# 615 products more on TensorE, in 41 patterns, that nothing reads

## The chip, the cores and the metric

The kernel runs on one core of one Trainium2 chip. The metric is the device time of one execution in microseconds. Two timed executions took 1457.32 and 1456.70 us, median 1457.01. A third was recorded by the hardware profiler.

In the profile PE is TensorE, the engine of matrix products, and PEld its weight loads; DVE is VectorE, ACT is ScalarE, POOL is GpSimd and SP is SyncE, which here only issues DMAs. A product on TensorE has a stationary operand, which a weight load brings into the array first, and a moving operand, whose columns are streamed through; the result is added up in PSUM.

## The reference

A trunk of two layers works on 272 tokens (16 learned ones and 256 real ones) of width 2048. Each layer ends in a residual and a layer norm.

```
for layer in range(DEPTH):                 # DEPTH = 2
    if layer % 2 == 0:
        f = _even_mixer(h, ...)            # gated linear attention and stick-breaking attention
    else:
        f = _odd_mixer(h, ...)             # Mamba-2 SSD mixer
    h = _layer_norm(DEEPNORM_ALPHA * h + f, ln_g[layer], ln_b[layer])
return h[:, PREFIX:]                       # the 256 real tokens
```

Both mixers are one wide input projection (2048 to some ten thousand columns), the mixing itself, a gate, and an output projection back to 2048. All of it is in float32. Most of the arithmetic is in the projections.

## The kernel before, in words

**Products.** A float32 operand is split into two parts, hi (rounded to the type fp32r, in which TensorE takes one pass over the columns) and lo (the rest). Every projection product is three products: hi times hi, hi times lo and lo times hi. The helper `three` (L161 to L165) issues them with the weights as stationary operand: `whi` with `xhi`, `whi` with `xlo`, `wlo` with `xhi`. So the first two have the same weights, and the moving operand has up to 272 columns, one per token. `out1_half` (L411 to L423), for the last output projection, does it the other way round: the activations `yh` and `yl` are stationary, and 512 (or 256) columns of weights are streamed.

**Operands.** `xhi` and `xlo` hold the layer's input for all 16 blocks of 128 input columns, 288 elements a row and block (`XW`), in fp32r. The weights come as units of 128 x 2048 elements by DMA into `raw`, three buffers; ACT makes `whi` of half a unit (L145), DVE or POOL makes `wlo` (L146), five buffers each. `self.parts[i, h]` names the parts of half h of unit i. `NU` is the number of units, so `NU - 1` is the last one.

**PSUM.** Four banks (`pj`) take the projections, two (`po`, L158 to L159) all smaller products in turn, and two (`zb`) serve the attention scores.

**Order.** The program is written as a list of units. While a unit's products are issued, generators for the mixing of earlier units are stepped on (`tick`), so that their instructions come in between. The order of each engine's instructions is then set by a planner, which goes by a simulated timeline and by priorities (program order, with some instructions marked as urgent): it takes the first instruction in priority that is ready. Waits between engines follow from what each instruction reads and writes. Each engine works off its own list in order.

**The end.** `tail` (L1087 to L1143) does the last four units by itself. The second and third of these are split not into `whi` and `wlo` but into the buffers of `xhi` and `xlo` (L1099, L1100), which nobody needs as input any more: elements 0 to 4095 of each row. The last unit is split as usual. Then come eight blocks of products, for two groups of 128 tokens and four groups of 512 output columns; DVE adds each block to the residual (L430) and takes its statistics (L1122). After the last block the second group of tokens is normalised on DVE, ACT and POOL (L1126 to L1141) and written out by three DMAs (L1142, L1143).

`setup` issues ten products of `ones` with `ones` before the first data is there (L231); nothing reads their result.

Of the kernel before, what the change touches and what calls it, by code (L numbers as in the profile page):

```python
# [12 lines left out]
P = 128  # L13
# [53 lines left out]
NU = len(L0) + len(L1)  # L67
# [20 lines left out]
class _Body:  # L88
# [998 lines left out]
    def tail(self):  # L1087

        nc, lp = self.nc, self.lp
        vec, pool = nc.vector, nc.gpsimd  # L1090
        i0, g = NU - 4, NG - 1
        self.drain()
        self.load_unit(i0 + 2)
        for n, dq in enumerate((1, 2)):
            for h in range(2):
                src = self.raw[i0 + dq][:, h * 1024 : (h + 1) * 1024]
                o = slice((2 * n + h) * 1024, (2 * n + h + 1) * 1024)
                hi, lo = [a.rearrange("p k t -> p (k t)")[:, o] for a in (self.xhi, self.xlo)]
                nc.scalar.activation(hi, src, AF.Copy)  # L1099
                vec.tensor_tensor(lo, src, hi.bitcast(F32), op=ALU.subtract)  # L1100
                self.parts[i0 + dq, h] = (hi, lo)
            if n == 0:
                self.load_unit(i0 + 3)
        lg = self.hp.tile([P, D], F32, tag="hacc", name="lg")
        lb = lp.tile([P, D], F32, tag="M", name="lb")
        nc.sync.dma_start(lg, self.lnr_d[0].partition_broadcast(P))
        nc.sync.dma_start(lb, self.lnr_d[1].partition_broadcast(P))
        for h in range(2):
            self.split_half(i0 + 3, h)
        for t in range(2):  # L1110
            st = lp.tile([P, 8, 6], F32, tag="fst", name=self.nm("fst"), bufs=2)
            acc = self.acc[:, t, :]
            for dq in range(4):
                halves = (0, 1) if t == 1 and dq == 3 else (None,)
                for b in halves:
                    ps = self.pj()
                    for h in range(2):
                        self.out1_half(ps, g, t, *self.parts[i0 + dq, h], h, b)
                    self.out1_add(ps, g, t, dq, b)
                    with self.tc.high_priority():  # L1120
                        for c in range(2) if b is None else (b,):
                            vec.bn_stats(st[:, 2 * dq + c, :], acc[:, dq * 512 + c * 256 : dq * 512 + (c + 1) * 256])  # L1122
            mv = lp.tile([P, 2], F32, tag="fmv", name=self.nm("fmv"), bufs=2)
            v, r, tm, mr = [lp.tile([P, 1], F32, tag=f"f{n}", name=self.nm("f"), bufs=2) for n in range(4)]
            with self.tc.high_priority():
                vec.bn_aggr(mv, st)  # L1126
                vec.tensor_scalar(v, mv[:, 1:2], LN_EPS, None, op0=ALU.add)
                nc.scalar.activation(r, v, AF.Ln)
                nc.scalar.activation(r, r, AF.Exp, scale=-0.5)
                self.newton(r, v, tm)  # L1130
                vec.scalar_tensor_tensor(mr, mv[:, 0:1], -1.0, r, op0=ALU.mult, op1=ALU.mult)
            cut = (0, 1024, 2048) if t == 0 else (0, 384, 1216, 2048)
            ch = [slice(a, b) for a, b in zip(cut, cut[1:])]
            for cs in ch[1:]:
                vec.scalar_tensor_tensor(acc[:, cs], acc[:, cs], mv[:, 0:1], lg[:, cs], op0=ALU.subtract, op1=ALU.mult)
            a = acc[:, ch[0]]
            nc.scalar.activation(a, a, AF.Identity, bias=mr, scale=r)
            pool.tensor_tensor(a, a, lg[:, ch[0]], op=ALU.mult)
            pool.tensor_tensor(a, a, lb[:, ch[0]], op=ALU.add)
            for cs in ch[1:]:  # L1140
                vec.scalar_tensor_tensor(acc[:, cs], acc[:, cs], r, lb[:, cs], op0=ALU.mult, op1=ALU.add)  # L1141
                nc.sync.dma_start(self.out[t * P : (t + 1) * P, cs], acc[:, cs])  # L1142
            nc.sync.dma_start(self.out[t * P : (t + 1) * P, ch[0]], a)  # L1143


def _pack(i):
# [53 lines left out]
```

## Time and profile before

| | us |
|---|---|
| median of two runs | 1457.01 |
| the profiled execution | 1456.58 |
| its span, first to last instruction | 1454.5 |
| PE busy | 1434.3 |
| DVE busy | 983.0 |
| ACT busy | 760.9 |
| POOL busy | 339.3 |

The granted clock of TensorE was 0.998 of full speed on average. A row of the timeline gives the start in us from the span's beginning, the length, the engine, the line, the operation, what it writes and reads with shapes, and how many it stands for. A group row gives the busy time and the mean length of one instruction in ns. Products overlap: the next starts before the last has ended. A row of the windows gives a stretch of the span, its length, and the busy time of each engine in it, with the number of instructions that lie in it at least partly.

### The profile page before, as it was taken

What the parts mean: (1) busy time and instruction counts of PE and PEld (TensorE: products, weight loads), DVE (VectorE), ACT (ScalarE), POOL (GpSimd) and SP (SyncE); (2) the same over time, 40 slices, a digit from 0 to 9 for tenths busy, and PEclk for the clock granted to TensorE, in tenths of its full rate; (3) what the DMA queues carried; (4) which work ended last, traced back from release to release, by engine and by line L of the source; (5) the groups of instructions that cost most, each with busy time, mean ns of one, the idle gap of its engine ahead of it and who ended that gap; (6) DMA issues with size and microseconds to landing.
All of it is one profiled execution on the core that took longest, in us unless ns stands there. A gap on an engine that the chain in (4) does not pass through costs nothing.

```text
span 1454.5 us, 26054 instructions
## 1 busy us (share of the span) xinstructions
PE 1434.3 (99%) x10780; PEld 1358.5 (93%) x10780; DVE 983.0 (68%) x1510; ACT 760.9 (52%) x1123; POOL 339.3 (23%) x297
## 2 busy tenths in 40 slices
PE   9999999999999999999989999999999999999997
PEld 7999999999999999999989999899898998989975
DVE  8646575574564454446897889577876767768677
ACT  6535454454335544445587566555555555555541
POOL 4000000000101010013502125433333433434323
PEclk9999999999999999999999999999999999999999
DMA  7644544444444444543435654554554555444551
GB/s 260 207 169 149 174 146 165 154 149 171 162 157 168 138 139 171 184 135 127 145 132 176 253 192 163 203 213 164 210 173 163 205 177 218 149 173 171 203 203 58
DMA packets 36566, 249.82 MB, mean 172 GB/s; under 512 B 4128, under 2 KB 4960, under 8 KB 7776
## 3 DMA queue, kind: packets, MB, share of 16 engines
q1 hardware_dynamic: 36304, 247.90, 48.5%
q8 instruction: 84, 1.38, 0.4%
q14 instruction: 34, 0.28, 0.1%
q10 hardware_dynamic: 144, 0.26, 0.1%
HBM read 245.94 MB, written 2.20 MB: 171 GB/s over the span
## 4 chain that ended last, share of the span: by engine, by line
PE 93%; DVE 4%; issue 1%; ACT 1%; POOL 1%; DMA 0%; POOLq 0%; SPq 0%; DVEq 0%
PE pj L163 24%; PE pj L165 24%; PE pj L164 23%; PE pj L421 4%; PE pj L423 4%; PE pj L422 4%; DVE wlo L146 1%; PE po L1053 1%; DVE xlo L735 1%; PE po L1055 1%; PE po L1007 1%; PE po L1057 0%; ACT whi L145 0%; DMA raw<-in_wts 0%; DVE hacc L836 0%
## 5 line engine op out<-in xcount | busy, mean ns | idle before, releaser
L163 PE MATMUL pj<-xhi,whi 128*128 128x272 f32 (+3 forms) x2560 | 738.9, 289 | 4.9 <-DVE fix L811 2.9
L165 PE MATMUL pj<-xhi,wlo 128*128 128x272 f32 (+3 forms) x2560 | 738.0, 289 | 0.0
L164 PE MATMUL pj<-xlo,whi 128*128 128x272 f32 (+3 forms) x2560 | 733.0, 286 | 1.9 <-DVE xlo L829 1.9
L146 DVE TENSOR_TENSOR wlo<-raw,whi 128x1024 fp32r<-128x1024 f32 (+1 forms) x402 | 511.6, 1275 | 301.1 <-ACT whi L145 298.6
L145 ACT ACTIVATE whi<-raw 128x1024 fp32r<-128x1024 f32 (+1 forms) x432 | 452.5, 1049 | 424.3 <-PE pj L164 358.3
L163 PEld LDWEIGHTS pj<-xhi,whi 128*128 128x128 f32 x2560 | 480.8, 188 | 9.2 <-issue 3.2
L164 PEld LDWEIGHTS pj<-xlo,whi 128*128 128x128 f32 x2560 | 482.0, 188 | 3.9 <-DVE xlo L829 2.4
L165 PEld LDWEIGHTS pj<-xhi,wlo 128*128 128x128 f32 x2560 | 480.8, 188 | 2.3 <-issue 1.5
L163 PE MATMUL pj<-mixh,whi 128*128 128x272 f32 x384 | 112.2, 294 | 0.0
L164 PE MATMUL pj<-mixl,whi 128*128 128x272 f32 x384 | 111.3, 290 | 0.0
L165 PE MATMUL pj<-mixh,wlo 128*128 128x272 f32 x384 | 110.9, 289 | 0.0
L146 POOL TENSOR_TENSOR wlo<-raw,whi 128x1024 fp32r<-128x1024 f32 x30 | 74.2, 2474 | 140.2 <-ACT whi L145 140.2
L421 PE MATMUL pj<-whi,yh 128*128 128x512 f32 (+1 forms) x244 | 98.2, 402 | 0.0
L423 PE MATMUL pj<-whi,yl 128*128 128x512 f32 (+1 forms) x244 | 96.0, 393 | 0.0
L422 PE MATMUL pj<-wlo,yh 128*128 128x512 f32 (+1 forms) x244 | 95.6, 392 | 0.0
L252 POOL TENSOR_TENSOR gr<-gr,gsc 128x1088 f32<-128x1088 f32 x6 | 15.4, 2574 | 294.8 <-ACT gsc L251 294.8
L163 PEld LDWEIGHTS pj<-mixh,whi 128*128 128x128 f32 x384 | 72.1, 188 | 0.5
L164 PEld LDWEIGHTS pj<-mixl,whi 128*128 128x128 f32 x384 | 72.3, 188 | 0.3
L165 PEld LDWEIGHTS pj<-mixh,wlo 128*128 128x128 f32 x384 | 72.3, 188 | 0.1
L430 DVE SCALAR_TENSOR_TENSOR acc<-pj,rr,acc 128x512 f32<-128x512 f32 (+1 forms) x65 | 47.4, 737 | 30.3 <-PE pj L423 30.3
L1061 POOL TENSOR_TENSOR yu<-yu,gz 128x256 f32<-128x256 f32 x32 | 39.2, 1233 | 80.0 <-DVE yu L1060 79.8
L423 PEld LDWEIGHTS pj<-whi,yl 128*128 128x128 f32 x244 | 46.0, 188 | 10.6
(302 smaller groups left out, 1507.6 us busy)
## 6 DMA issues: line engine op xcount, KB each, us to landing
raw<-in_wts SPq DMA_DIRECT2D x214, 1024.0 KB, 4.8
ebc<-edr SPq DMA_DIRECT2D x8, 1664.0 KB, 6.5
hacc<-in_xT SPq DMA_DIRECT2D x8, 272.0 KB, 6.4
raw<-in_wts SPq DMA_DIRECT2D x8, 256.0 KB, 5.4
lg<-in_lnr SPq DMA_DIRECT2D x1, 1024.0 KB, 4.3
lb<-in_lnr SPq DMA_DIRECT2D x1, 1024.0 KB, 6.0
out_h<-acc SPq DMA_DIRECT2D x2, 512.0 KB, 2.6
out_h<-acc SPq DMA_DIRECT2D x2, 416.0 KB, 2.5
```

The costliest lines, as they stand in the source:

```text
L145: self.nc.scalar.activation(hi, src, AF.Copy)
L146: eng.tensor_tensor(lo, src, hi.bitcast(F32), op=ALU.subtract)
L163: mm(ps, whi, xhi, start=first, stop=False)
L164: mm(ps, whi, xlo, start=False, stop=False)
L165: mm(ps, wlo, xhi, start=False, stop=last)
L252: mul(c, c, e, op=ALU.mult)
L421: mm(ps, yh[:, kk, tt], hi[:, k, :], start=kk == 0, stop=False)
L422: mm(ps, yh[:, kk, tt], lo[:, k, :], start=False, stop=False)
L423: mm(ps, yl[:, kk, tt], hi[:, k, :], start=False, stop=kk == 3)
L430: self.nc.vector.scalar_tensor_tensor(a, ps, r[:, t : t + 1], a, op0=ALU.mult, op1=ALU.add)
L735: vec.scalar_tensor_tensor(self.xlo[:, d, :T], x, g, self.xhi[:, d, :T].bitcast(F32), op0=ALU.mult, op1=ALU.subtract)
L1061: nc.gpsimd.tensor_tensor(u, u, z[:, j, :], op=ALU.mult)
```

## The change

`tail` gets one more line, a call of a new function `rest`. That issues 41 patterns of 15 products each behind the needed ones. A pattern takes one of the two `po` banks and adds 15 products up in it, five groups of three as in `three`; nothing reads the bank afterwards. Stationary are the first half of the last unit's parts (or two constant 128 x 128 arrays), moving are parts of `xhi` and `xlo`, which by then hold weights.

The patterns differ in the number of moving columns (`n`: 27 patterns with 272, six with 256, five with 512, and one each with 264, 288 and 384), in where the moving operands start (`xo`, `xlo`) and by how much they advance from group to group (`pitch`), in where the weights start (`wo`, `wlo`), whether they advance (`wp`), how many of their columns are used (`m`), whether their elements lie side by side or 2, 4 or 8 apart (`step`), in the order of the three products (`order`), and in whether the moving columns are read backwards (`back`). The output of the kernel is the same as before.

```diff
             nc.sync.dma_start(self.out[t * P : (t + 1) * P, ch[0]], a)
+        self.rest()
+
+    def rest(self):
+
+        mm = self.nc.tensor.matmul
+        xh, xl = [a.rearrange("p k t -> p (k t)") for a in (self.xhi, self.xlo)]
+        wh, wl = self.parts[NU - 1, 0]
+
+        def pattern(n, xo=0, xlo=None, wo=0, wlo=None, pitch=288, wp=P, m=P, step=1, order=0, st=None, mv=None, rep=5, back=False):
+            ps = self.po()
+            xlo = xo if xlo is None else xlo
+            wlo = wo if wlo is None else wlo
+            for k in range(rep):
+                a, b = st or (wh, wl)
+                if step == 1:
+                    hi, lo = [t[:, o + k * wp : o + k * wp + m] for t, o in ((a, wo), (b, wlo))]
+                else:
+                    hi, lo = [t[:, o + k : o + k + step * (m - 1) + 1 : step] for t, o in ((a, wo), (b, wlo))]
+                c, d = mv or (xh, xl)
+                p, q = [t[:, o + k * pitch : o + k * pitch + n] for t, o in ((c, xo), (d, xlo))]
+                if back:
+                    p, q = p[:, ::-1], q[:, ::-1]
+                seq = [[(hi, p), (hi, q), (lo, p)], [(hi, q), (hi, p), (lo, p)], [(hi, p), (lo, p), (hi, q)]][order]
+                for i, (s, v) in enumerate(seq):
+                    self.nc.tensor.matmul(ps[:m, :n], s, v, start=k == 0 and i == 0, stop=k == rep - 1 and i == 2)
+
+        pattern(272)
+        pattern(272, pitch=0)
+        pattern(272, pitch=0, wp=0)
+        pattern(272, mv=(xh, xh))
+        pattern(272, st=(self.ones_r, self.nL_r), wp=0)
+        pattern(272, st=(self.ones_r, self.ones_r), wp=0)
+        for o in (16, 32, 48):
+            pattern(272, pitch=320, xo=o)
+        pattern(272, pitch=320)
+        for o in (16, 32, 48):
+            pattern(272, pitch=320, xlo=o)
+        for o in (16, 32, 48):
+            pattern(272, pitch=320, wlo=o)
+        pattern(272, pitch=320, wo=32, wlo=0)
+        pattern(272, pitch=320, step=2)
+        pattern(272, pitch=320, step=4)
+        pattern(272, pitch=320, step=8)
+        pattern(272, pitch=320, back=True)
+        pattern(272, pitch=320, order=1)
+        pattern(272, pitch=320, order=2)
+        pattern(272, pitch=288, order=2)
+        pattern(272, pitch=320, m=64)
+        pattern(272, pitch=320, wp=112, m=112)
+        pattern(272, pitch=384)
+        for o in (0, 16, 32, 48):
+            pattern(256, pitch=320, xo=o)
+        pattern(256, pitch=320, step=8)
+        pattern(256, pitch=320, order=2)
+        pattern(264, pitch=320)
+        pattern(288, pitch=320)
+        for o in (0, 16, 32, 48):
+            pattern(512, pitch=512, xo=o)
+        pattern(512, pitch=512, step=8)
+        pattern(384, pitch=512)
```

## The prediction

> **What bounds the kernel now.** I read the page first, its busy times and its chain of waits, to see which engine sets the end.
>
> ```profile
> span 1454.5 us, 26054 instructions
> PE 1434.3 (99%) x10780; PEld 1358.5 (93%) x10780; DVE 983.0 (68%) x1510; ACT 760.9 (52%) x1123; POOL 339.3 (23%) x297
> ...
> PE 93%; DVE 4%; issue 1%; ACT 1%; POOL 1%; DMA 0%; POOLq 0%; SPq 0%; DVEq 0%
> ...
> L163 PE MATMUL pj<-xhi,whi 128*128 128x272 f32 (+3 forms) x2560 | 738.9, 289 | 4.9 <-DVE fix L811 2.9
> ...
> L163 PEld LDWEIGHTS pj<-xhi,whi 128*128 128x128 f32 x2560 | 480.8, 188 | 9.2 <-issue 3.2
> ```
>
> TensorE (PE) is busy in 1434.3 of 1454.5 us and carries 93% of the chain that ended last. There is one weight load for each product (10780 and 10780), also where two products in a row have the same weights. The mean of 289 ns is the length of one product from start to end; products overlap, so it isn't the price of one. The price is the distance between two starts, and I take that below from the timeline.
>
> Next I divided the end of the span into windows: before the last eight blocks of products, during them, and after them.
>
> ```profile
> 1409.00:1420.90 11.90, 11.90 (x54) 9.66 (x53) 11.75 (x14) 7.92 (x10) 2.72 (x2) 1.00 0.53 178
> 1420.90:1443.50 22.60, 22.60 (x109) 18.61 (x108) 16.08 (x34) 1.66 (x3) 6.98 (x3) 1.00 0.06 23
> 1443.50:1454.50 11.00, 0.11 (x1) 0.00 (x0) 6.70 (x12) 1.11 (x3) 3.86 (x3) 0.70 0.36 143
> ```
>
> The columns are the window, its length, then busy time and count of PE, PEld, DVE, ACT and POOL, the granted clock, the DMA share and GB/s. PE has no gap up to 1443.5 (22.60 of 22.60 us). Then it has nothing to do for 11 us, while DVE, ACT, POOL and the output DMAs finish the last layer norm. Those 11 us are all the free room that the change can find behind the needed products. The timeline gives the two ends of it, and the DMA view of the last 4.5 us gives the landing of the last output:
>
> ```profile
> 1440.64 0.28 PE L421 MATMUL pj<-whi,yh 128*128 128x256 f32 x1
> ...
> 1443.34 0.28 PE L423 MATMUL pj<-whi,yl 128*128 128x256 f32 x1
> 1443.65 0.48 DVE L430 SCALAR_TENSOR_TENSOR acc<-pj,rr,acc 128x256 f32<-128x256 f32 x1 [0.42 <-PE pj L423]
> ...
> 1451.44 0.33 SPq L1143 DMA_DIRECT2D out_h<-acc  x1
> ```
> ```profile
> out_h<-acc SPq DMA_DIRECT2D x1, 192.0 KB, 2.1
> ```
>
> The last DMA is issued at 1451.44 and lands 2.1 us later, at 1453.54; the span ends 0.96 us after that. This 0.96 us is what the program needs from its last piece of work to its end. The profiled execution took 1456.58 us, 2.08 more than its span; the median of the two timed runs is 1457.01, 0.43 above it.
>
> **Price of one product, by column count.** First and last rows of stretches without a gap:
>
> ```profile
> 565.33 0.29 PE L165 MATMUL pj<-xhi,wlo 128*128 128x272 f32 x1
> ...
> 574.45 0.29 PE L165 MATMUL pj<-xhi,wlo 128*128 128x272 f32 x1
> ```
> ```profile
> 681.33 0.29 PE L165 MATMUL pj<-mixh,wlo 128*128 128x272 f32 x1
> ...
> 690.43 0.29 PE L165 MATMUL pj<-mixh,wlo 128*128 128x272 f32 x1
> ```
> ```profile
> 1423.30 0.39 PE L422 MATMUL pj<-wlo,yh 128*128 128x512 f32 x1
> ...
> 1432.44 0.39 PE L422 MATMUL pj<-wlo,yh 128*128 128x512 f32 x1
> ```
> ```profile
> 565.50:574.50 9.00, 9.00 (x73) 9.00 (x73) 4.22 (x5) 3.07 (x4) 0.00 (x0) 1.00 0.33 118
> 681.50:690.50 9.00, 9.00 (x73) 9.00 (x73) 9.00 (x13) 8.26 (x16) 8.76 (x9) 1.00 0.35 119
> ...
> 1398.50:1407.50 9.00, 9.00 (x40) 7.26 (x39) 9.00 (x12) 5.82 (x9) 5.35 (x5) 1.00 0.65 214
> 1423.50:1432.50 9.00, 9.00 (x40) 7.21 (x39) 4.61 (x10) 0.00 (x0) 0.00 (x0) 1.00 0.00 0
> ```
>
> The first stretch holds 73 products of 272 columns, so 72 distances: 9.12 / 72 = 126.7 ns. The second, 73 too: 9.10 / 72 = 126.4 ns. I take 126.5. The third holds 40 of 512 columns: 9.14 / 39 = 234.4 ns. From 1440.64 to 1443.34, in the fence before, are 24 products of 256 columns: 2.70 / 23 = 117.4 ns. One column more costs (234.4 - 117.4) / 256 = 0.457 ns.
>
> The windows show what does not matter: the same 73 products fit into 9 us with DVE, ACT and POOL nearly full (9.00, 8.26, 8.76) and with them at less than half, and the same 40 with the DMA engines at 0.65 and at 0.00. So the added products will not become cheaper because the rest of the chip is quiet while they run. The two 272-column stretches also read from layouts of different pitch (288 and 272 elements a row) at one price.
>
> **The change, part by part.** It removes nothing and moves nothing in the program's text; it adds 41 x 15 = 615 products with 615 weight loads on PE, no DMA and no work for another engine. By column counts in the diff: 27 patterns have 272 columns, 6 have 256, 5 have 512, one each 264, 288 and 384.
>
> - 405 products of 272: 405 x 0.1265 = 51.2 us.
> - 90 of 256: 90 x 0.1174 = 10.6 us.
> - 75 of 512: 75 x 0.2344 = 17.6 us.
> - 15 each of 264 (between 256 and 272: 122 ns), 288 (126.5 + 16 x 0.457 = 133.8) and 384 (117.4 + 128 x 0.457 = 175.9): 15 x 0.4317 = 6.5 us.
>
> Together 85.9 us of PE. At those distances the weight loads are covered, as they are in the stretches above, which have one each.
>
> Where do they run? They read the two big operand buffers, which the tail overwrites with weights, and the parts of the very last weight unit:
>
> ```profile
> 1418.83 1.21 DVE L1100 TENSOR_TENSOR xlo<-raw,xhi 128x1024 fp32r<-128x1024 f32 x1
> 1419.96 1.22 DVE L146 TENSOR_TENSOR wlo<-raw,whi 128x1024 fp32r<-128x1024 f32 x1
> ```
>
> The last part that nearly all of them need is written by 1421.18. By then PE has, without a gap, the last eight blocks of needed products before it, and all inputs of these are there. So most patterns come behind 1443.46 (1443.34 + 0.117), or between the needed products; either way PE's work adds up to the same sum. The last product, one of 384 columns, starts at 1443.46 + 85.9 - 0.18 = 1529.2, lasts some 0.34 (between the 0.28 and 0.39 of the rows) and ends at 1529.5. With the 0.96 us of the program's end the span is 1530.5, and with the 2.08 around it 1532.5: 76 us above the profiled execution, of 85.9 added, because 10 lie beside the layer norm that used to be alone at the end. What was the end before is done at 1454.5 and then no longer matters, unless the needed products are pushed back.
>
> Costs that the trace does not show as such:
> - Weights read with a step of 2, 4 or 8 elements (5 patterns, 75 products). No load in the trace has a step. Below: no cost, the load stays covered. Above: it isn't covered at all, and its 188 ns are added: 14.1 us. I take nothing: the covered loads are the nearest rows.
> - Columns read backwards (15 products): between nothing and a doubled price, 1.9 us. Nothing taken.
> - The change of the result buffer from pattern to pattern. There are two, nobody reads the results, so a pattern waits at most for one of its own engine. If PE had to empty each time, it would lose the part of a product that overlaps the next, 289 - 126 = 163 ns, 41 times: 6.7 us. The needed blocks change their buffers too, inside the stretch without a gap, so nothing taken.
> - Fetching 1230 more instructions. All of PE's idle time outside the last 11 us is 1454.5 - 1434.3 - 10.9 = 9.3 us for 10780 products, 0.9 ns each: at most 0.5 us.
> - A gain: addresses at which a product gets cheaper. Neighbouring rows show distances that differ:
>
> ```profile
> 507.47 0.28 PE L163 MATMUL pj<-xhi,whi 128*128 128x272 f32 x1
> 507.59 0.28 PE L164 MATMUL pj<-xlo,whi 128*128 128x272 f32 x1
> 507.71 0.30 PE L165 MATMUL pj<-xhi,wlo 128*128 128x272 f32 x1
> 507.85 0.29 PE L163 MATMUL pj<-xhi,whi 128*128 128x272 f32 x1
> ```
>
> ```profile
> 1442.64 0.28 PE L423 MATMUL pj<-whi,yl 128*128 128x256 f32 x1
> 1442.75 0.28 PE L421 MATMUL pj<-whi,yh 128*128 128x256 f32 x1
> ```
>
> The first rows lie 0.12, 0.12 and 0.14 us apart, so single distances swing by some per cent about 126.5; the last two, of 256 columns, lie 0.11 apart, 6.3% under their mean of 0.1174. If all patterns lay at that short end, it would be 85.9 x 0.063 = 5.4 us less. I take the mean.
> - 64 or 112 result rows instead of 128: the row below has 64 and lasts as long (295 ns against 289), so no gain.
>
> ```profile
> L163 PE MATMUL po<-xhi,whi 128*64 128x274 f32 x16 | 4.7, 295 | 0.7 <-ACT xhi L734 0.7
> ```
>
> **The rivals.**
>
> First, the products run faster than the needed ones. The price of 126.5 ns for 272 columns may hold a surplus that depends on how the two operands lie to each other, and many patterns lie otherwise. For it speaks the swing just shown, against it that two pitches give one price. By the short end of that swing the time is 1532.5 - 5.4 = 1527.1. The Trainium skill, TensorE: Matmul & The Clock Gate, section Back-to-back issue gap, gives N / 2.4 + 2.5 ns for a warm product of N columns, 115.8 ns for 272: my estimate from it for all 615 is 78.9 us, and the time 1525.5. The trace disagrees for the needed products: 126.5, 117.4 and 234.4 ns where the rule has 115.8, 109.2 and 215.8. That section also names 131 ns a product at 512 columns in a stream, which no row here comes near. The chance of this rival is 0.08.
>
> Second, some addresses cost much. The strided loads, the backwards read and the change of buffers at their upper ends add 14.1 + 1.9 + 6.7 = 22.7 us, to 1555. For it speaks only that no row has these forms. Chance 0.10, most of it below 1543, as all three would have to be at their worst.
>
> Third, the planner sets the patterns ahead of needed products. It does let PE's order differ from the program's:
>
> ```profile
> 1408.80 0.39 PE L422 MATMUL pj<-wlo,yh 128*128 128x512 f32 x1
> ...
> 1409.03 0.61 PE L1076 MATMUL po<-ones,ysq 128*128 128x128 f32 x4
> ...
> 1409.40 0.48 PE L423 MATMUL pj<-whi,yl 128*128 128x512 f32 x1
> ```
>
> There another task's products stand inside a group of three. Each us of patterns set ahead pushes the layer norm back by one, but the end only moves when 1454.5 plus the part set ahead passes 1530.5, that is from 76 of the 85.9 us on. With all ahead: 1454.5 + 85.9 + 2.08 = 1542.5. Against it speaks that nearly all wait for the write that ends at 1421.18. Chance 0.04.
>
> Fourth, on the other side: the products cost nothing, because what nobody reads is dropped when the program is built. Then the time stays at 1456.6, and this decides as soon as no more than some 70 products are left (1454.5 - 0.96 - 0.34 - 1443.46 = 9.7 us, at 85.9 / 615 = 0.14 us each). Against it stands the warm-up of the kernel itself, ten products that nobody reads, which are there as twenty:
>
> ```profile
> L231 PE MATMUL po<-ones x20: 274/421/580, 1.1 to 4.6; 128*128 128x128 f32 x20
> ```
>
> Chance 0.03.
>
> **How the numbers follow.** The forecast, 1532.5 us with its own range of 1529 to 1536, has 0.74; the rivals have 0.08, 0.10, 0.04 and 0.03; 0.01 is left for something unnamed that makes the kernel faster. The range reaches to the short end of the swing below (1527) and to the planner's case above (1543), which takes in the part of the costly addresses up to 10 us. About 2% is what a measurement of this kernel can tell from no change; of 1457 that is 29 us, and every case but the fourth and the unnamed one lies beyond it on the slow side: slower 0.96, within 2% 0.03, faster 0.01.
>
> **What would show it.** In the changed kernel's page PE has 11395 products and as many loads, and the chain ends in PE at the lines of the added function, with the output DMAs landing some 75 us before the end. The windows after 1443.5 show PE full, the other engines at nothing from about 1455 on, and the granted clock at 1.00. The timeline gives distances near 126.5, 117.4 and 234.4 ns in every pattern; a pattern with a stepped load at 150 ns or more would be the second rival, a pattern at 120 or less the first. Needed products that end later than 1443.6 would show the planner's mixing, and an end of the layer norm near 1530 the third rival. The prediction is wrong if the sum of the distances leaves 80 to 96 us, or if the end is not set by PE.

## The result, and the profile after

The changed kernel takes 1537.51 us (median of two runs, 1537.35 and 1537.68), 80.5 us more than 1457.01. The ratio is 1.0549, with a 95% interval of 1.0532 to 1.0566. The forecast was 1532.5 us, with a range of 1527 to 1543.

The page of the changed kernel, its span, busy times and chain of waits:

```profile
span 1535.3 us, 27284 instructions
PE 1526.3 (99%) x11395; PEld 1447.3 (94%) x11395; DVE 982.7 (64%) x1510; ACT 761.3 (50%) x1123; POOL 339.1 (22%) x297
...
PE 94%; DVE 4%; issue 1%; ACT 1%; POOL 0%; DMA 0%; SPq 0%; DVEq 0%; POOLq 0%
PE pj L163 23%; PE pj L165 23%; PE pj L164 22%; PE po L1168 6%; PE pj L421 4%; PE pj L423 4%; PE pj L422 4%; DVE wlo L146 1%; PE po L1053 1%; DVE xlo L735 1%; PE po L1055 1%; PE po L1007 1%; PE po L1057 0%; ACT whi L145 0%; DMA raw<-in_wts 0%
```

All 615 products are there (11395 instead of 10780) with as many weight loads; the other engines have the same counts as before and are busy as long. The added line, L1168, is 6% of the chain that ended last. The windows of the end show where it lies:

```profile
1420.90:1443.50 22.60, 22.60 (x109) 18.67 (x108) 16.12 (x34) 1.65 (x3) 6.73 (x3) 1.00 0.06 24
1443.50:1454.50 11.00, 11.00 (x90) 11.00 (x89) 6.72 (x12) 1.12 (x3) 4.13 (x3) 1.00 0.36 143
1454.50:1535.30 80.80, 79.90 (x530) 77.00 (x529) 0.00 (x0) 0.00 (x0) 0.00 (x0) 1.00 0.00 1
```

During the eight last blocks of needed products PE is as full as before (22.60 of 22.60 us, with 109 products in both). The 11 us in which PE had nothing to do are now full, beside the same work on DVE, ACT and POOL (6.72, 1.12 and 4.13 us, before 6.70, 1.11 and 3.86). Then PE works alone for 80 us, at full clock. The timeline of PE gives the ends:

```profile
1443.54 0.28 PE L423 MATMUL pj<-whi,yl 128*128 128x256 f32 x1
1443.65 0.29 PE L1168 MATMUL po<-xhi,whi 128*128 128x272 f32 x1
...
1534.06 0.34 PE L1168 MATMUL po<-xhi,wlo 128*128 128x384 f32 x1
```

No added product stands ahead of a needed one. From the first added start to the last are 90.4 us, and with the last product's own distance of 0.17 the 615 take 90.6 us, where the forecast had 85.9. The last one ends at 1534.40, and the span 0.9 us later. Four patterns carry more than the whole difference, and the timeline shows three of them as a step in the distances:

```profile
1475.66 0.29 PE L1168 MATMUL po<-xhi,whi 128*128 128x272 f32 x1
...
1477.56 0.39 PE L1168 MATMUL po<-xhi,whi 128*128 128x272 f32 x1
...
1481.07 0.40 PE L1168 MATMUL po<-xhi,whi 128*128 128x272 f32 x1
...
1484.69 0.29 PE L1168 MATMUL po<-xhi,whi 128*128 128x272 f32 x1
...
1486.56 0.29 PE L1168 MATMUL po<-xlo,whi 128*128 128x272 f32 x1
...
1504.90 0.40 PE L1168 MATMUL po<-xhi,whi 128*128 128x256 f32 x1
...
1508.53 0.28 PE L1168 MATMUL po<-xhi,whi 128*128 128x256 f32 x1
```

Each pair of neighbouring rows up to 1486.56 bounds one pattern of 15 products, and so does the pair from 1504.90 to 1508.53. With weights read at a step of 2 it takes 1.90 us (127 ns a product), at a step of 4 3.51 us (234 ns), at a step of 8 3.62 us (241 ns); then the backwards columns take 1.87 us (about 124 ns by the single starts). The 256 columns at a step of 8 take 3.63 us (242 ns), as much as 272. The rows of the weight loads, around the start of the pattern with a step of 4 and in that with a step of 8, tell why:

```profile
1477.31 0.19 PEld L1168 LDWEIGHTS po<-xhi,wlo 128*128 128x128 f32 x1
1477.43 0.31 PEld L1168 LDWEIGHTS po<-xhi,whi 128*128 128x128 f32 x1
1477.64 0.33 PEld L1168 LDWEIGHTS po<-xlo,whi 128*128 128x128 f32 x1
...
1481.17 0.34 PEld L1168 LDWEIGHTS po<-xlo,whi 128*128 128x128 f32 x1
```

The first row belongs to a load with a step of 2, the next two to a step of 4, the last to a step of 8. A load lasts 0.31 to 0.34 us instead of 0.19. A product of 272 columns no longer covers it: its distance rises with the load.

### The profile page after: what moved, and what is told of

The parts are those of the page before. It is cut to its first block, busy times and chain, and to the rows that moved or that the text cites. A ratio compares the mean times of both kernels' runs of the same rounds, so it can differ in the third digit from the quotient of the medians.

```text
span 1535.3 us, 27284 instructions
## 1 busy us (share of the span) xinstructions
PE 1526.3 (99%) x11395; PEld 1447.3 (94%) x11395; DVE 982.7 (64%) x1510; ACT 761.3 (50%) x1123; POOL 339.1 (22%) x297
## 4 chain that ended last, share of the span: by engine, by line
PE 94%; DVE 4%; issue 1%; ACT 1%; POOL 0%; DMA 0%; SPq 0%; DVEq 0%; POOLq 0%
PE pj L163 23%; PE pj L165 23%; PE pj L164 22%; PE po L1168 6%; PE pj L421 4%; PE pj L423 4%; PE pj L422 4%; DVE wlo L146 1%; PE po L1053 1%; DVE xlo L735 1%; PE po L1055 1%; PE po L1007 1%; PE po L1057 0%; ACT whi L145 0%; DMA raw<-in_wts 0%
## 5 line engine op out<-in xcount | busy, mean ns | idle before, releaser
L1168 PE MATMUL po<-xhi,whi 128*128 128x272 f32 (+7 forms) x200 | 61.0, 310 | 0.0
L1168 PE MATMUL po<-xhi,wlo 128*128 128x272 f32 (+7 forms) x195 | 60.5, 311 | 0.0
```

The source lines that it names most:

```text
L1168: self.nc.tensor.matmul(ps[:m, :n], s, v, start=k == 0 and i == 0, stop=k == rep - 1 and i == 2)
```

## The experiments

**The stepped loads alone.** The five patterns with a step get a step of 1; nothing else differs.

```diff
-        pattern(272, pitch=320, step=2)
-        pattern(272, pitch=320, step=4)
-        pattern(272, pitch=320, step=8)
+        pattern(272, pitch=320)
+        pattern(272, pitch=320)
+        pattern(272, pitch=320)
...
-        pattern(256, pitch=320, step=8)
+        pattern(256, pitch=320)
...
-        pattern(512, pitch=512, step=8)
+        pattern(512, pitch=512)
```

> The five patterns whose weights were read with a step of 2, 4 or 8 elements read them side by side; the number of products and columns stays. Theory A (a stepped load is longer than the product that should cover it, and that is all that the forecast missed): the three 272-column ones fall to about 126 ns a product, the 256-column one to 118, the 512-column one to 234; 15 x (0.234 - 0.126) + 15 x (0.242 - 0.126) + 15 x (0.2415 - 0.118) + 15 x (0.244 - 0.234) = 5.4 us less than the changed kernel: 1532.1 us. Rival B (the 5 us came with the change of the result bank or with fetching instructions, and fall on these patterns by chance): 1537.5 us, and other patterns show gaps.

Measured: 1531.97 us, ratio to the kernel before (1456.92 beside it) 1.0517 (1.0502 to 1.0533); 5.5 us less than the changed kernel, and 0.5 us from the forecast of 1532.5. In its timeline the pattern that had a step of 4 lies between these rows:

```profile
1477.39 0.29 PE L1168 MATMUL po<-xhi,whi 128*128 128x272 f32 x1
...
1479.28 0.29 PE L1168 MATMUL po<-xhi,whi 128*128 128x272 f32 x1
```

That is 1.89 us for 15 products, 126 ns each. No other pattern shows a gap in either kernel, so rival B falls. Theory A holds: the stepped loads are what the forecast had missed.

**The room beside the last layer norm.** Two kernels keep only the first patterns.

```diff
         pattern(272)
         pattern(272, pitch=0)
         pattern(272, pitch=0, wp=0)
         pattern(272, mv=(xh, xh))
-        pattern(272, st=(self.ones_r, self.nL_r), wp=0)
...
```

> Only the first four patterns, 60 products, behind the needed ones. Theory A (there is room beside the last layer norm up to about 1453.6 less 0.3): 60 x 0.1254 = 7.5 us end at 1451.3, so the time is that of the kernel before, 1457.0 us. Rival B (no room; work on PE behind the needed products always adds, since the layer norm is slowed or the end waits for PE otherwise): 1457.0 + 7.5 = 1464.5 us.

Measured: 1457.52 us (median of ten, from 1456.80 to 1460.26), ratio 1.0007 (0.9997 to 1.0017): no difference that can be measured. In its profile, whose span is 1455.7 us, the last added product ends at 1452.3.

The second keeps five patterns more:

```diff
         pattern(272, st=(self.ones_r, self.nL_r), wp=0)
         pattern(272, st=(self.ones_r, self.ones_r), wp=0)
         for o in (16, 32, 48):
             pattern(272, pitch=320, xo=o)
-        pattern(272, pitch=320)
...
```

> Only the first nine patterns, 135 products. Theory A: 135 x 0.1256 = 17.0 us from 1443.65, end of the last product at 1460.8, span 1461.7, time 1463.8 us: 6.8 us more than before, of 17.0 added. Rival B (no room): 1474.0 us.

Measured: 1463.64 us, ratio 1.0046 (1.0031 to 1.0061), 6.7 us more than the 1456.92 of the kernel before beside it. Its windows:

```profile
1443.50:1454.50 11.00, 11.00 (x90) 11.00 (x90) 6.72 (x12) 1.12 (x3) 4.15 (x3) 1.00 0.36 143
1454.50:1461.70 7.20, 6.28 (x50) 6.06 (x49) 0.00 (x0) 0.00 (x0) 0.00 (x0) 1.00 0.00 0
```

Of the 17 us of products some 10 lie beside the layer norm, which is done in its 6.72, 1.12 and 4.15 us as before, and the rest comes behind it. The room is there, and it has the size that the forecast read from the idle time of PE.

**The patterns ahead of the needed products.** The call moves to a place before the last eight blocks.

```diff
         for h in range(2):
             self.split_half(i0 + 3, h)
+        self.rest()
         for t in range(2):
...
-        self.rest()
```

> All 41 patterns, called ahead of the last eight blocks of needed products instead of behind them. Theory A (the layer norm at the end is the only work that the patterns lie beside): nothing lies beside them now, and the time is 1457.0 + 90.4 (the sum of the distances in the changed kernel) = 1547.4 us, 10 us above the changed kernel. Rival B (the end is PE's sum of work in any order): 1537.5 us.

Measured: 1540.39 us, ratio 1.0574 (1.0558 to 1.059), which is neither number. The timeline shows an order that neither theory had in mind:

```profile
1515.38 0.39 PE L1168 MATMUL po<-xhi,wlo 128*128 128x512 f32 x1
1515.61 0.28 PE L423 MATMUL pj<-whi,yl 128*128 128x256 f32 x1
...
1515.96 0.28 PE L423 MATMUL pj<-whi,yl 128*128 128x256 f32 x1
1516.08 0.39 PE L1168 MATMUL po<-xhi,whi 128*128 128x512 f32 x1
...
1527.11 0.28 PE L423 MATMUL pj<-whi,yl 128*128 128x256 f32 x1
1527.23 0.52 PE L1168 MATMUL po<-xhi,whi 128*128 128x512 f32 x1
```

The planner mixed the two: mostly five needed products, then two patterns (30 products), and so on, until 585 of the 615 stood ahead of the last needed one. That one starts at 1527.11 instead of 1443.54, 83.6 us later, with two patterns (30 products) still behind it. The chain of waits then leaves PE there:

```profile
1527.27 0.13 PE pj L423
...
1527.43 0.49 DVE acc L430
```

Before + what stands ahead is 1456.9 + 83.6 = 1540.5 us, and 1540.39 was measured. So theory A's mechanism holds for the part that was really ahead (each us set ahead pushes the layer norm by one), and its number fell because not all was. Theory B falls: the end is PE's sum only as long as the layer norm is done sooner.

**How long a load takes at each step.** In place of the 41 patterns stand sets of 15 equal products; all read their columns from one place.

```diff
...
+        def probe(n, so=0, mo=0, m=P, step=1, s=wh, v=xh):
+            ps = self.po()
+            for k in range(15):
+                mm(ps[:m, :n], s[:, so : so + step * (m - 1) + 1 : step], v[:, mo : mo + n], start=k == 0, stop=k == 14)
+
+        for step in (1, 2, 3, 4, 5, 6, 7, 8, 12, 16, 32):
+            probe(64, step=step, s=xh, v=xl)
+        for step in (2, 4, 8):
+            probe(64, step=step, m=64, s=xh, v=xl)
+        for step in (1, 2, 3, 4, 5, 6, 7, 8, 16):
+            probe(256, step=step, s=xh, v=xl)
```

> In place of the 41 patterns: sets of 15 equal products with the weights read at steps of 1 to 32 elements, with 64 columns (where the load and not the stream should set the price) and with 256; three sets with only 64 weight columns. Theory A (the price is the longer of stream and load, and a load takes longer the farther its elements lie apart): at 256 columns 118 ns at steps 1 and 2, something between 126 and 234 at step 3, 234 at 4, 235 to 242 at 5 to 16. Theory B (only steps that are powers of two collide): steps 3, 5, 6 and 7 at 118 ns, 4, 8 and 16 at 234 to 242. With 64 columns both expect the load alone: at most 118 ns at step 1, the same 234 and 242 at steps 4 and 8; with 64 weight columns half of that, about 117 and 121. Theory C (load and stream add up): 64 columns at step 8 well below 256 columns at step 8.

This run and the two behind it are one execution each, read for the distances in them and not for their times. The timeline joins equal neighbours in one row. Its length runs from the first start to the last end, so the distance is that length less one product's, divided by the count less one. Sets of 256 columns, those with steps of 4, 5, 7, 8 and 16, and then the one with a step of 3:

```profile
1490.69 3.20 PE L1155 MATMUL po<-xlo,xhi 128*128 128x256 f32 x13
1493.96 3.36 PE L1155 MATMUL po<-xlo,xhi 128*128 128x256 f32 x14
...
1501.05 3.22 PE L1155 MATMUL po<-xlo,xhi 128*128 128x256 f32 x13
1504.83 3.12 PE L1155 MATMUL po<-xlo,xhi 128*128 128x256 f32 x12
1508.26 3.04 PE L1155 MATMUL po<-xlo,xhi 128*128 128x256 f32 x13
```
```profile
1487.73 2.72 PE L1155 MATMUL po<-xlo,xhi 128*128 128x256 f32 x15
```

A product lasts 0.34 us at step 3 and 0.38 to 0.41 at the others, so the distances are 234 ns at step 4, 228 at 5, 235 at 7, 246 at 8 and 221 at 16. The row of step 3 begins with the last product of the set before it, 0.12 us ahead of the first of its own: (2.72 - 0.34 - 0.12) / 13 = 174 ns. The set with a step of 2 came at 120, by its single starts, and that with 6 at 228. Theory B falls: 3, 5, 6 and 7 are not as cheap as 2. Of A the first half holds, the price is the longer of stream and load; the second, that a load gets longer the farther its elements lie apart, holds only up to step 4. Behind it the price stays between 220 and 250, and 5, 6 and 16 lie below the 235 to 242 that were expected. Why it levels off there, no run shows. Theory C falls by the changed kernel itself: at a step of 8, 256 and 272 columns cost the same 242 and 241 ns.

The sets of 64 columns tell less of the steps than was meant, because the clock changed under them. The windows of this kernel:

```profile
1443.70:1448.00 4.30, 4.30 (x38) 4.30 (x36) 3.90 (x11) 0.41 (x2) 1.22 (x1) 1.00 0.30 122
1448.00:1449.00 1.00, 1.00 (x7) 1.00 (x6) 1.00 (x3) 0.71 (x1) 0.11 (x1) 0.60 0.00 0
1449.00:1485.00 36.00, 36.00 (x180) 36.00 (x180) 1.81 (x2) 0.00 (x0) 2.58 (x2) 0.50 0.08 30
1486.00:1511.00 25.00, 25.00 (x121) 25.00 (x120) 0.00 (x0) 0.00 (x0) 0.00 (x0) 1.00 0.00 1
```

The granted clock fell to 0.50 some 5 us after the first product of 64 columns and came back only after the sets of 256 had begun, although PE and PEld count as busy throughout. At the half clock the sets with steps of 4 to 8 cost 223 to 238 ns, near what 256 columns cost at full clock, and with 64 weight columns those of 4 and 8 cost 118 and 120, half as much, as expected. Only the first two sets of 64 columns, at steps 1 and 2, ran wholly at full clock:

```profile
1443.83 1.39 PE L1155 MATMUL po<-xlo,xhi 128*128 128x64 f32 x11
1445.40 1.58 PE L1155 MATMUL po<-xlo,xhi 128*128 128x64 f32 x12
```

With some 0.28 us for one product they give 111 ns at step 1 and 118 at step 2: the load alone. Both lie under the 126 of a 272-column product, so step 2 cost nothing in the changed kernel.

**Where the operands lie.** The same `probe` with four starts of the weights (`so`) and several of the columns (`mo`).

```diff
...
+        for so in (0, 16, 32, 48):
+            for mo in range(0, 64, 8):
+                probe(256, so, mo)
+        for so in (0, 16, 32, 48):
+            for mo in (0, 16, 32, 48):
+                probe(512, so, mo)
```

> In place of the 41 patterns: sets of 15 equal products, 256 columns with four starts of the weights by eight starts of the columns, 512 columns with four by four. Theory A (the price depends on how the columns lie to the weights of the next load): between 113 and 121 ns at 256 and between 226 and 235 at 512, with equal prices where the difference of the two starts is equal. Theory B (on the start of the columns alone): the same eight prices for each start of the weights. Theory C (on neither): all within 1 ns of 117.4 and 234.4.

Four sets of 512 columns, with starts of weights and columns at (0, 16), (0, 48), (16, 0) and (16, 16), so with differences, modulo 64, of 16, 48, 48 and 0 elements:

```profile
1504.47 2.92 PE L1155 MATMUL po<-xhi,whi 128*128 128x512 f32 x12
...
1511.40 2.97 PE L1155 MATMUL po<-xhi,whi 128*128 128x512 f32 x12
1514.90 2.96 PE L1155 MATMUL po<-xhi,whi 128*128 128x512 f32 x12
1518.40 2.90 PE L1155 MATMUL po<-xhi,whi 128*128 128x512 f32 x12
```

With 0.39 us for one product they are 230, 234, 234 and 228 ns. Over whole sets, from the single starts in the trace without the first two distances, the means at a difference of 0 are 227.0 to 227.7 ns for all four starts of the weights, at 16 they are 229.1 (and 229.8 once), at 32 231.7 to 232.6, at 48 233.3 in all four. At 512 columns theory A holds: what counts is how the columns lie to the weights. At 256 columns most sets lie between 117 and 120 ns, at a difference of 0 at 120 for all four starts of the weights; of the four with a difference of 48 three settle at 113 after some products and one stays at 118, so the difference alone doesn't set the price there, and what else does stays open.

**Columns, weight columns and bytes.**

```diff
...
+        for n in (64, 96, 128, 160, 192, 224, 256, 272, 320, 384, 448, 512):
+            probe(n)
+        for m in (32, 64):
+            for n in (128, 256, 272, 512):
+                probe(n, m=m)
+        sb, vb = [self.lp.tile([P, 1024], mybir.dt.bfloat16, tag="bc", name=self.nm("pb"), bufs=2) for _ in range(2)]
+        for d, e in ((sb, wh), (vb, xh)):
+            self.nc.vector.tensor_copy(d, e[:, :1024].bitcast(F32))
+        for n in (128, 256, 272, 512):
+            probe(n, s=sb, v=vb)
```

> In place of the 41 patterns: sets of 15 equal products with 64 to 512 columns, with 32 and 64 weight columns instead of 128, and with operands in bf16 instead of fp32r. A line through the prices of the kernel before (117.4 ns at 256, 234.4 at 512) goes through zero nearly: 0.457 ns a column. Theory A (the price is the longer of stream and load): 0.457 ns a column from about 230 columns up, and a flat 105 to 110 below. Theory B (no floor from the load): 29 ns at 64 columns, 58 at 128. Whether the weight loads cause the part of the 0.457 that lies above the faster patterns: if they do, 32 weight columns bring 256 columns to 113 ns or less and 512 to 227 or less; if not, 117 and 234 stay. Operands of half the bytes: if reading 4 bytes a column is what is slow, 256, 272 and 512 columns fall to about 109, 116 and 216 ns. These last three are what the Trainium skill, TensorE: Matmul & The Clock Gate, section Back-to-back issue gap, gives by its formula.

From the timeline, fp32r with 64, 192, 256 and 512 columns, 256 and 512 columns with 32 weight columns, and bf16 with 256, 272 and 512:

```profile
1444.52 1.28 PE L1155 MATMUL po<-xhi,whi 128*128 128x64 f32 x10
1451.04 1.63 PE L1155 MATMUL po<-xhi,whi 128*128 128x192 f32 x13
1454.79 1.36 PE L1155 MATMUL po<-xhi,whi 128*128 128x256 f32 x10
...
1466.23 3.15 PE L1155 MATMUL po<-xhi,whi 128*128 128x512 f32 x13
...
1470.58 1.42 PE L1155 MATMUL po<-xhi,whi 128*32 128x256 f32 x11
1474.19 3.16 PE L1155 MATMUL po<-xhi,whi 128*32 128x512 f32 x13
...
1486.32 1.36 PE L1155 MATMUL po<-pb,pb 128*128 128x256 bf16 x11
1487.85 1.44 PE L1155 MATMUL po<-pb,pb 128*128 128x272 bf16 x11
1490.02 2.75 PE L1155 MATMUL po<-pb,pb 128*128 128x512 bf16 x12
```

The lengths of one are 0.27, 0.28, 0.28 and 0.39 us, with 32 weight columns 0.28 and 0.39, and 0.27, 0.28 and 0.38 in bf16. So 64 and 192 columns cost the same 112 ns, the load (theory A, which had 105 to 110; all sets from 64 to 224 columns have means of 111.6 to 111.9 without the first two distances). That it is the load is seen where fewer weight columns are loaded: 128 columns with 32 or 64 weight columns cost 60 ns, by their single starts. 512 columns cost 230 ns whether 128 or 32 weight columns are loaded with them, so there the loads are not what makes the fp32r columns slow. At 256 columns they have a part: 120 ns with 128 weight columns, 114 with 32 or 64, which is neither of the two outcomes that were expected (113 or less, or 117). In bf16 the prices are 109, 116 and 216 ns. Those are what the Trainium skill, TensorE: Matmul & The Clock Gate, section Back-to-back issue gap, gives by its formula N / 2.4 + 2.5 for a single warm product of 256, 272 and 512 columns (109.2, 115.8 and 215.8). The rule holds here for operands in bf16, of 2 bytes, in a stream with one load each; those in fp32r, of 4 bytes, cost mostly 5 to 9% more. Type and bytes changed together, for both operands, so which of them sets the price stays open.

## Why the prediction was right, point by point

**The place.** All 615 products came behind the needed ones, with no gap before or between, at a clock of 1.00, on PE alone. As predicted, PE sets the end and 10 us lie beside the layer norm; its last output is issued at 1451.69 and, with the 2.1 us to its landing, is there at 1453.8, long before the end. One sign of the prediction was set too tight: the last needed product ends at 1443.82, later than 1443.6, though none was mixed in. Its start differs from run to run, from 1443.34 in the kernel before to 1444.53 in the one with four patterns, with no added product ahead of it in either. The two kernels with fewer patterns show the room from both sides of its edge, and that of the patterns called ahead shows the price if it is lost, one us for one.

**The number.** The forecast's own range of 1529 to 1536 was missed by 1.5 us. The time lies in the wider range because that was stretched to 1543, the time of the third rival, which did not happen. The prediction said that this also takes in costly addresses up to 10 us, and such a cost is what came; that the range reached far enough is in part luck.

**The sum.** The products took 90.6 us where the forecast had 85.9. By its terms, from the starts in the trace: 25 patterns of 272 columns without the slow steps came at 125.5 ns (126.5 predicted), the five of 256 at 117.8 (117.4), the four of 512 at 231.1 (234.4), and 264, 288 and 384 at 120, 131.5 and 174 (122, 133.8 and 175.9). That is 0.6 us less than forecast, a part of which the run with other starts explains: at 512 columns the price depends on where the two operands lie, from 227 to 233 ns.

**The term that was mis-sized** is the weights read with a step, where the forecast gave bounds of 0 and 14.1 us and took nothing, "the covered loads are the nearest rows". Four of its five patterns were not covered. Their cost over the same patterns without a step is 5.5 us by the two times (1537.51 and 1531.97). The reason behind the 0 was the wrong step: the loads of the trace were covered because each takes less than its product (112 ns by itself in the later runs, against 126), and that says nothing of how long a load with a step takes. Nor is the upper bound's mechanism right, the load's 188 ns added to the product: the price is the longer of the two, 234 to 242 ns for 256 and 272 columns and 244 for 512. So the extra is the price of the load less that of the product, 108 to 124 ns at 256 and 272 columns and 10 at 512.

**The other unknowns** came out at the value taken: backwards columns at 124 ns, 64 and 112 result rows at 124 and 126, and between two patterns of 272 columns, where the result bank changes, no distance above 135 ns where the loads have no slow step. The gain from better addresses exists and is small, as the first rival's section had it from two neighbouring rows; one set of 256 columns in the changed kernel (columns from 48 on) came at 113.7 ns, near the 0.11 us quoted there. The end took 0.9 us after the last product (0.96 predicted).

**The rivals.** The second, that some addresses cost much, had 0.10 and is what moved the time by 5 us, within its bounds, through the stepped loads alone; its sign, a stepped load at 150 ns or more, was seen. The first had the right mechanism, prices that depend on how the operands lie, but not its size, since the added products came on average within 1.5% of the needed ones. The third did not happen, but the planner does mix when the call stands earlier in the program, and its price was right: by the prediction's way, with 83.6 us ahead, 1454.5 + 83.6 + 2.08 = 1540.2, and 1540.39 was measured. The fourth fell with the count of 11395.

## What to carry to other kernels

Before pricing a product, ask which of its two halves sets the distance between starts, the stream of columns or the load of the next weights; a layout that changes only the load can double the price. In these runs weights whose 128 columns lie side by side or two apart were covered by 256 columns of fp32r; those three or more apart were not, and at 512 columns a step of 8 still cost some 10 ns. Work added to the busiest engine is free only up to the time that it idles at the end, and only if the planner leaves it behind what others wait for: read both from the order of that engine's starts.

## What the runs showed of the hardware that was not expected

The price of a load by step is not in proportion: 111 and 118 ns at steps 1 and 2, 174 at 3, 234 at 4, then 228, 235, 246 and 221 at 5, 7, 8 and 16.

In the run with the steps, products of 64 columns that lay 111, 118 and 173 ns apart were followed by a fall of the granted clock from 1.00 to 0.50, for some 36 us, though PE counts as busy throughout. In the run with the columns, sets of 64 to 224 columns, 112 ns apart, kept a clock of 1.00 over 10 us, so the distance alone isn't what counts; what does, these two executions don't show. The Trainium skill, TensorE: Matmul & The Clock Gate, Part 1, says that the clock is granted by how busy PE has been lately, with half speed as the other state; the 0.50 agrees, and the busy time of the profile can't be the measure.

At 512 columns of fp32r the price depends on the difference between the starts of columns and weights: 227 ns where it is 0, 233 where it is 48 elements. And operands in bf16 stream at 216 ns for 512 columns where those in fp32r take 227 to 235, whether 128 or 32 weight columns are loaded; at 256 columns fewer weight columns brought 120 down to 114.
